# Where in memory the attention and feed-forward activations begin: a two-layer float32 decoder on one core

## The chip, the cores and the metric

One core of one Trainium2 chip runs one program. The metric is the device time of an execution in microseconds, as the median of several runs; lower is better. Engine names are those of the profile: PE is TensorE (PEld are its weight loads), DVE is VectorE, ACT is ScalarE, POOL is GpSimd and SP is SyncE, which issues nearly all transfers.

## The reference

Two layers (`DEPTH = 2`) on 512 tokens of width 1024, all in float32. Each layer is an attention sub-layer and a SwiGLU sub-layer, each with an RMSNorm ahead of it and one behind it:

```
h = rms_norm(x, attn_pre_g[l])
proj = h @ w_in[l]                       # q, k, v of 4 differential heads and 8 forgetting heads
oa = rms_norm(diff_attention(qa, ka, va, lam), diff_sub_g[l]) * (1.0 - lam_init)
ob = forgetting_attention(qb, kb, vb, log_f)
x = x + rms_norm(concat(oa, ob) @ w_out[l], attn_post_g[l])
h = rms_norm(x, ffn_pre_g[l])
y = (silu(h @ w_gate[l]) * (h @ w_up[l])) @ w_down[l]      # D_FF = 2816
x = x + rms_norm(y, ffn_post_g[l])
```

## The kernel before

**Three matmuls for one.** Each float32 operand is split into a high part that is rounded to the matmul's type and a low part with the rest, and each product is the sum of three matmuls (high by high, high by low, low by high). In `mm(out, a, b)` (line 204) `a` is the stationary operand, 128x128, loaded by a weight load (LDWEIGHTS), and `b` the moving one, up to 512 columns wide. A profile row such as `d<-wh_d,hh` names the output and both operands.

**The work of a layer, in order.** `va` (lines 333 to 342) makes the values of the differential heads: the stationary operand is a 128-token slice of the normed input `hT_h` or `hT_l`, the moving one a half-width row block of the weights. Then come the projections `pj_kd`, `pj_qd`, `pj_kf`, `pj_qf` and `vb`, the scores `sd` and `sf`, the transposes of the probabilities `ptd` and `ptf`, and the products with the values, `od` and `of`. A planner (`Plan`) fixes their order at build time; projections and the output projection `o` fill the gaps that the softmax leaves on PE. After that the order is the program's: the output projection's rest, gate and up (`pj_g`, `pj_u`, function `proj_T`: the stationary operand is a weight tile, the moving one `hT_h` or `hT_l`), and down (`d`, function `down_mm`: the stationary operand is a 128-token slice of the hidden activations `hh` or `hl`, the moving one a weight tile). Down has 22 row blocks, 2 halves of the width, 4 token tiles and 3 matmuls each, so 528 matmuls of 512 columns in a layer.

**Weights.** They arrive by a transfer of 512 KB in `wr` (two buffers), ACT writes the high part `wh` and DVE or POOL the low part `wl` (three buffers each). Four rows of down's weights at its end (`TAIL`) lie in free tiles of the feed-forward pool instead (`whl`), and so do the values' weights of the second layer (`wvh`, `wvl`, loaded through `vraw`). In the first layer three quarters of the values' weights lie in tiles of the attention pool (`wva`, `wva0h`, `wva0l`), loaded through `mixd` and `rawv`, and the last quarter in the weight pool (`wh_va`, `wl_va`). Half of the output projection's weights lie in the attention pool too (`wo1h`, `wo1l`), the other half in the weight pool (`wh_o`, `wl_o`).

**Where tiles lie.** A pool is a stretch of SBUF; pools lie one behind the other in the order of their creation, and the attention pool `att{l}` and the feed-forward pool `ffn{l}` take turns in the last stretch. All tiles that matter here are multiples of 512 bytes long in each partition, and a slice of 128 tokens is 512 bytes, so an operand's offset, which here means its start address modulo 512 bytes, is that of its pool. In the compiled program before the change the offsets are:

| tiles | pool | offset |
|---|---|---|
| `xs`, `hT_h`, `hT_l`, the identity in `con` | cpool | 128 |
| `wr`, `wh`, `wl` of all weights | wpool | 384 |
| normed rows `h`, exponentials `ed` and `ae`, `sg` | tpool | 384 |
| `mixd`, `rawv`, `vdh`, `vdl`, `vf`, `wo1h`, `wo1l`, `wva`, `qs`, `ks` | att | 256 |
| `t1`, `t2`, `cb`, `pth`, `ptl` | att | 128 |
| `hh`, `hl`, `whl`, `wvh`, `wvl`, `vraw`, `y0` | ffn | 256 |

The pad tile of `PAD = 8` floats at the end of the small pool `spool` is what puts the last stretch at 256.

Of the kernel before, what the change touches and what calls it, by code (L numbers as in the profile page):

```python
# [11 lines left out]
F32 = mybir.dt.float32  # L12
# [5 lines left out]
P = 128  # L18
# [21 lines left out]
EPS = 1e-6  # L40
BIG = 1e30
MAGIC = 12582912.0
PAD = 8
C_ID, C_M, C_F, NKEEP, C_U = 0, 128, 640, 641, 641
NCONST = 1153
PAIRED = [*range(8, 16), *range(8), *range(16, 32)]
# [127 lines left out]
def hymba_block(ctx, tc, x_d, pos_d, apre_d, win_d, fb_d, lq1_d, lk1_d, lq2_d, lk2_d, dsg_d, wout_d, apost_d,  # L174
# [51 lines left out]
    dsg = cpool.tile([P, DEPTH], F32, name="dsg")  # L226
    spool.tile([P, PAD], F32, name="pad", tag="pad", bufs=1)

# [114 lines left out]
    for l in range(DEPTH):  # L343
        win = win_d[l]
        with ExitStack() as actx:
            ap = actx.enter_context(tc.tile_pool(name=f"att{l}", bufs=1, reuse_waits="tile"))

            def rbuf(tag, dt, name):
                return ap.tile([P, S], dt, name=f"{name}_{l}", tag=tag, bufs=NRC if tag == "rc" else 1)
# [982 lines left out]
```

## Time and profile before

| | us |
|---|---|
| median of 3 runs | 1267.25 (1266.63 to 1270.36) |
| the profiled execution | 1271.73 |
| its span | 1270.0 |
| PE busy in it | 1233.9 (97%) |
| weight loads (PEld) | 1017.4 (80%) |
| DVE, ACT, POOL busy | 635.0 (50%), 520.6 (41%), 279.4 (22%) |

The mean granted clock of TensorE is 0.992 of full speed. The profiled execution took 4.48 us longer than the median; 1.73 us of its time lie outside the span. A matmul's duration in the profile (0.39 us for 512 columns) overlaps that of the next; what counts is the distance from the start of one to the start of the next.

### The profile page before, as it was taken

The numbers are of one execution on the slowest core, as the hardware profiler recorded it, in microseconds if no ns is written. First come the engines' busy times: TensorE is split into PE (matmuls) and PEld (weight loads), VectorE is DVE, ScalarE is ACT, GpSimd is POOL, SyncE is SP. The second block draws the span as 40 slices with busy tenths as digits, with TensorE's granted clock in tenths as the row PEclk, the third lists the DMA queues.
The fourth block names the chain that finished last, engine by engine and source line by source line (L and its number), as shares of the span: only waits on it lengthen the run. The fifth ranks groups of instructions, "written<-read, shape, count | busy, mean of one in ns | idle before, by whom it ended". The sixth has DMA issues, their size and how long they took to land.

```text
span 1270.0 us, 15915 instructions
## 1 busy us (share of the span) xinstructions
PE 1233.9 (97%) x5949; PEld 1017.4 (80%) x5949; DVE 635.0 (50%) x1188; ACT 520.6 (41%) x1008; POOL 279.4 (22%) x318
## 2 busy tenths in 40 slices
PE   8999999999999999999999999999999999999998
PEld 5777887798888888888777878777988888888886
DVE  7597859563333333221556867685633333332224
ACT  5465757453222222222344647674522222221211
POOL 1554557220000000000236535671100000000001
PEclk9999999999999999999999999999999999999999
DMA  7333443404333334223413333432133333332222
GB/s 235 82 84 93 108 116 101 133 18 116 90 94 99 100 100 133 85 97 101 132 34 92 80 95 102 124 128 81 51 100 100 100 92 93 99 117 100 83 100 83
DMA packets 158717, 125.94 MB, mean 99 GB/s; under 512 B 7008, under 2 KB 134112, under 8 KB 158640
## 3 DMA queue, kind: packets, MB, share of 16 engines
q1 hardware_dynamic: 158496, 124.40, 33.0%
q8 instruction: 47, 0.77, 0.2%
q10 hardware_dynamic: 144, 0.52, 0.1%
q14 instruction: 30, 0.25, 0.1%
HBM read 114.32 MB, written 2.20 MB: 92 GB/s over the span
## 4 chain that ended last, share of the span: by engine, by line
PE 55%; issue 31%; DVE 7%; ACT 3%; POOL 3%; DMA 1%; SPq 0%; POOLq 0%; DVEq 0%; ACTq 0%
PE pj_g L204 9%; PE pj_u L204 9%; PE d L204 9%; PE o L204 4%; PE pj_kd L204 4%; PE pj_qd L204 3%; PE va L204 3%; PE vb L204 2%; PE pj_kf L204 2%; PE pj_qf L204 2%; PE sd L204 1%; PE ptf L209 1%; PE sf L204 1%; PE of L204 1%; DVE ae L1032 1%
## 5 line engine op out<-in xcount | busy, mean ns | idle before, releaser
L204 PE MATMUL pj_g<-hT_h,wh_g 128*128 128x512 f32 (+1 forms) x384 | 142.9, 372 | 0.0
L204 PE MATMUL pj_g<-hT_h,wl_g 128*128 128x512 f32 (+1 forms) x384 | 142.6, 371 | 0.0
L204 PE MATMUL pj_g<-hT_l,wh_g 128*128 128x512 f32 (+1 forms) x384 | 142.6, 371 | 0.0
L204 PE MATMUL pj_u<-hT_h,wh_u 128*128 128x512 f32 (+1 forms) x368 | 140.1, 381 | 0.0
L204 PE MATMUL pj_u<-hT_h,wl_u 128*128 128x512 f32 (+1 forms) x368 | 139.8, 380 | 0.0
L204 PE MATMUL pj_u<-hT_l,wh_u 128*128 128x512 f32 (+1 forms) x368 | 139.8, 380 | 0.0
L204 PE MATMUL d<-wh_d,hh 128*128 128x512 f32 x336 | 132.6, 395 | 0.0
L204 PE MATMUL d<-wh_d,hl 128*128 128x512 f32 x336 | 132.6, 395 | 0.0
L204 PE MATMUL d<-wl_d,hh 128*128 128x512 f32 x336 | 132.5, 394 | 0.0
L258 DVE TENSOR_TENSOR wl_u<-wr_u,wh_u 128x1024 fp32r<-128x1024 f32 x44 | 53.9, 1225 | 150.5 <-ACT wh_u L257 150.5
L258 DVE TENSOR_TENSOR wl_d<-wr_d,wh_d 128x1024 fp32r<-128x1024 f32 x42 | 51.5, 1225 | 152.0 <-ACT wh_d L257 151.5
L257 ACT CAST wh_u<-wr_u 128x1024 fp32r<-128x1024 f32 x44 | 46.3, 1052 | 158.4 <-PE pj_g L204 151.7
L257 ACT CAST wh_d<-wr_d 128x1024 fp32r<-128x1024 f32 x42 | 44.1, 1049 | 162.4 <-PE d L204 139.1
L257 ACT CAST wh_g<-wr_g 128x1024 fp32r<-128x1024 f32 x44 | 46.4, 1055 | 145.2 <-issue 124.6
L1205 DVE TENSOR_TENSOR sg<-pj_u,sg 128x512 f32<-128x512 f32 x44 | 30.4, 692 | 140.8 <-PE pj_u L204 140.8
L270 POOL TENSOR_SCALAR v_fp<-s_fp 128x1 f32<-128x1 f32 x8 | 4.1, 508 | 370.4 <-ACT junk L276 370.1
L204 PEld LDWEIGHTS pj_g<-hT_h,wh_g 128*128 128x128 f32 x384 | 72.4, 188 | 12.7
L204 PEld LDWEIGHTS pj_g<-hT_l,wh_g 128*128 128x128 f32 x384 | 72.3, 188 | 12.5
L204 PEld LDWEIGHTS pj_g<-hT_h,wl_g 128*128 128x128 f32 x384 | 72.3, 188 | 12.4
L204 PEld LDWEIGHTS pj_u<-hT_h,wl_u 128*128 128x128 f32 x368 | 69.3, 188 | 13.1
L204 PEld LDWEIGHTS pj_u<-hT_l,wh_u 128*128 128x128 f32 x368 | 69.2, 188 | 13.0
L204 PEld LDWEIGHTS pj_u<-hT_h,wh_u 128*128 128x128 f32 x368 | 69.2, 188 | 13.1
(272 smaller groups left out, 2777.8 us busy)
## 6 DMA issues: line engine op xcount, KB each, us to landing
wr_g<-in_w_gate_dram SPq DMA_DIRECT2D x44, 512.0 KB, 3.8
wr_u<-in_w_up_dram SPq DMA_DIRECT2D x44, 512.0 KB, 3.8
wr_d<-in_w_down_dram SPq DMA_DIRECT2D x44, 512.0 KB, 3.5
wr_o<-in_w_out_dram SPq DMA_DIRECT2D x16, 512.0 KB, 4.2
wr_kd<-in_w_in_dram SPq DMA_DIRECT2D x8, 512.0 KB, 4.0
wr_qd<-in_w_in_dram SPq DMA_DIRECT2D x8, 512.0 KB, 4.1
ksd<-ksd SPq DMA_DIRECT2D x16, 256.0 KB, 2.9
wr_kf<-in_w_in_dram SPq DMA_DIRECT2D x8, 512.0 KB, 4.0
```

Of the source, the lines that this page charges most:

```text
L204: ins = PE.matmul(out, a, b, start=start, stop=stop)
L209: ins = PE.transpose(out, a, idn)
L257: A.copy(hi, raw)
L258: (eng or V).tensor_sub(lo, raw, hi.bitcast(F32))
L270: G.tensor_scalar(v, s2[:, 0:1], scalar1=s2[:, 1:2], scalar2=EPS, op0=ALU.add, op1=ALU.add)
L1032: return V.tensor_scalar_mul(b["e"][:, :n], b["e"][:, :n], b["l"])
L1205: V.tensor_mul(sg, pu, sg)
```

## The change

The pad in `spool` grows from 8 to 104 floats, by 384 bytes, and the attention pool gets a pad tile of 64 floats, 256 bytes, as its first one. Nothing else is changed.

```
-PAD = 8
+PAD, PAD_A = 104, 64
...
             ap = actx.enter_context(tc.tile_pool(name=f"att{l}", bufs=1, reuse_waits="tile"))
+            ap.tile([P, PAD_A], F32, name=f"pad_a{l}", tag="pad")
```

In the compiled program the feed-forward pool then begins at byte 135808 in place of 135424, and its tiles have the offset 128. The attention pool's first real tile begins at 136064 in place of 135424; its tiles that had the offset 256 have 384, and those that had 128 have 256. The other pools stay where they were. Tiles of the two pools now overlap at other places than before, and the order in which instructions are issued is the same on all engines. One wait moves. On DVE, where the second layer's attention begins (`vdl` are the low parts of the values, `t1kd` the first step of the key rotation, `hT_l` the normed input's low part), the rows before are:

```order
L263 TENSOR_TENSOR hT_l<-hp_a_5583,hT_h 128x4x128 [waits Activation_49]
L382 TENSOR_TENSOR vdl_5646<-va_5498,vdh_5645 128x512 [waits DMAHW3_49,Activation_49]
...
L727 TENSOR_TENSOR t1kd_1_5718<-pj_kd_5678,cosT 128x512 [waits DMAHW6_49,PE_49]
L731 STREAM_SHUFFLE t2kd_1_5723<-pj_kd_5678 128x512 [waits DMAHW0_49]
L734 TENSOR_TENSOR t2kd_1_5723<-t2kd_1_5723,sinT 128x512 [waits DVE_49]
```

and with the change:

```order
L263 TENSOR_TENSOR hT_l<-hp_a_5584,hT_h 128x4x128 [waits Activation_49]
L383 TENSOR_TENSOR vdl_5648<-va_5499,vdh_5647 128x512 [waits DMAHW6_49,DMAHW3_49,Activation_49]
...
L728 TENSOR_TENSOR t1kd_1_5720<-pj_kd_5680,cosT 128x512 [waits PE_49]
L732 STREAM_SHUFFLE t2kd_1_5725<-pj_kd_5680 128x512 [waits DMAHW0_49]
L735 TENSOR_TENSOR t2kd_1_5725<-t2kd_1_5725,sinT 128x512 [waits DVE_49]
```

The wait on DMAHW6, which is for the landing of one of the eight `vraw` transfers, moved from `t1kd` to the first `vdl`, four rows earlier.

## Rows read from the trace of the kernel before

**Rows 1.** The page's part 1: engine, busy us, share of the span, instructions.

```profile
PE 1233.9 (97%) x5949; PEld 1017.4 (80%) x5949; DVE 635.0 (50%) x1188; ACT 520.6 (41%) x1008; POOL 279.4 (22%) x318
```

**Rows 2.** Busy time by stretch: gate and up, then down, first layer.

```profile
core 0: us, PE busy (x) PEld busy (x) DVE busy (x) ACT busy (x) POOL busy (x), PEclk, DMA share, GB/s
271.00:513.00 242.00, 242.00 (x1145) 203.61 (x1145) 88.40 (x98) 73.15 (x97) 2.36 (x5) 1.00 0.33 98
513.00:638.00 125.00, 124.52 (x541) 100.78 (x540) 39.70 (x40) 34.58 (x53) 9.55 (x12) 1.00 0.32 102
```

**Rows 3.** The chain of waits, its long pieces: start us, us, what, count.

```profile
242.51 17.42 PE o L204 x75
262.20 4.18 PE o L204 x18
268.65 2.80 PE o L204 x12
...
502.62 5.44 PE pj_g L204 x24
...
513.51 114.33 PE d L204 x492
653.07 11.16 PE va L204 x48
...
870.22 10.48 PE o L204 x45
```

**Rows 4.** Timeline of PE, values of the first layer: start us, us, instruction.

```profile
21.95 0.39 PE L204 MATMUL va<-wva,hT_l 128*128 128x512 f32 x1
...
32.40 0.40 PE L204 MATMUL va<-wva,hT_l 128*128 128x512 f32 x1
32.64 0.40 PE L204 MATMUL va<-wh_va,hT_h 128*128 128x512 f32 x1
...
34.73 0.39 PE L204 MATMUL va<-wh_va,hT_h 128*128 128x512 f32 x1
...
38.13 0.39 PE L204 MATMUL pj_kd<-hT_h,wh_kd 128*128 128x512 f32 x1
```

**Rows 5.** Timeline of PE at the end of the second layer's down.

```profile
1258.71 0.61 PE L204 MATMUL d<-whl,hh 128*128 128x512 f32 x2
1259.16 0.39 PE L204 MATMUL d<-whl,hl 128*128 128x512 f32 x1
1259.39 0.40 PE L204 MATMUL d<-wh_d,hh 128*128 128x512 f32 x1
...
1260.78 0.63 PE L204 MATMUL d<-whl,hh 128*128 128x512 f32 x2
```

**Rows 6.** The chain of waits between the layers, last pieces ahead of PE.

```profile
649.72 0.76 DVE h_a L285
650.48 0.14 issue
650.62 0.63 PE hp_a L209 x4
```

**Rows 7.** Timelines of DVE and PE, last normed rows ahead of the second feed-forward.

```profile
905.28 0.75 DVE L285 SCALAR_TENSOR_TENSOR h_f<-xs,r_f,g_fpre 128x512 f32<-128x512 f32 x1 [1.99 <-POOL r_f L271]
906.93 0.60 PE L209 MATMUL hp_f<-con,h_f 128*128 128x128 f32 x4
```

**Rows 8.** Transfers: their issues with KB each and median us to landing; timelines of users.

```profile
wr_d<-in_w_down_dram SPq DMA_DIRECT2D x44, 512.0 KB, 3.5
ksd<-ksd SPq DMA_DIRECT2D x16, 256.0 KB, 2.9
vraw<-in_w_in_dram SPq DMA_DIRECT2D x8, 256.0 KB, 3.8
51.08 2.17 SPq L709 DMA_DIRECT2D ksd<-ksd  x2
59.45 0.30 PEld L204 LDWEIGHTS sd<-ksd,qsd 128*128 128x128 f32 x2 [1.86 <-issue]
607.42 2.37 SPq L1281 DMA_DIRECT2D vraw<-in_w_in_dram  x4
```

**Rows 9.** The first low part of the second layer's values: duration, first and last start.

```profile
L382 DVE TENSOR_TENSOR vdl<-va,vdh x4: 681/687/693, 660.8 to 664.9; 128x512 fp32r<-128x512 f32 x4
```

## The prediction

> **What bounds the kernel now.** I read first the busy times: PE is busy for 97% of the span and no other compute engine for more than half of it [rows 1]. Then the stretches: in gate and up and in down PE has no gap to speak of, the granted clock is 1.00, and the 16 transfer engines are busy a third of the time [rows 2]. So in the feed-forward the time is the number of matmuls times the distance between two of them. The third view, the chain of waits, gives that distance. A piece of gate and up is 24 matmuls of 512 columns in 5.44 us, 226.7 ns each. Down is 492 matmuls of the same size in 114.33 us, 232.4 ns each [rows 3]. The clock is the same, the other engines and the transfers do no more in down than in gate and up [rows 2], and still every matmul of down takes 5.7 ns longer. The reader should ask what differs: which operand lies where.
>
> The offsets in the table of pools answer it. In gate and up the stationary operand has the offset 384 and the moving one 128. In down it is 256 and 384. The trace holds a direct comparison in one stretch, one loop and one clock, the values of the first layer [rows 4]. From 21.95 us to 32.64 us 46 matmuls read their moving operand from the attention pool (offset 256, stationary operand at 128): 10.69 us, 232.4 ns each. At 32.64 us the same loop goes on with its moving operand in the weight pool (offset 384, stationary still at 128). The first nine take 2.09 us, 232.2 ns each, and the next 15, up to 38.13 us, take 3.40 us, 226.7 ns each. Nothing else changed but the tile. A third case lies at the end of down: with `whl` both operands are in the feed-forward pool, both at 256, and the three from 1258.71 to 1259.39 us take 0.68 us, 226.7 ns each; the six that follow with `wh_d` (256 and 384) take 1.39 us, 231.7 ns [rows 5]. And the output projection, with `wo1h` at 256 moving and 128 stationary, runs at 17.42 / 75 = 232.3 ns [rows 3].
>
> So the rule that the rows show: where the two operands' offsets are equal or 256 apart, a matmul settles at 226.7 ns after about nine; where they are 128 apart, it stays at 232.4 ns on average.
>
> **The change part by part.** It takes no instruction away and adds none; it moves the offsets of two pools. *Down*: stationary from 256 to 128, moving stays at 384, so 256 apart. That is the pair of operand offsets of the 15 fast matmuls in [rows 4]. In each layer 480 matmuls run ahead of the last token loop: 480 x 5.7 ns = 2.74 us, both layers 5.48. In that last loop of the second layer 24 more read `wh_d`: 24 x 5.0 = 0.12 us. In the first layer only the first six of these count, 0.03 us; the rest is covered by the chain of norms, in which PE's transposes wait for DVE's `h_a` up to 650.62 us [rows 6]. Sum 5.6 us, all of it on PE without gaps, so on the path.
>
> *Output projection*: moving `wo1h` and `wo1l` from 256 to 384, stationary 128, 256 apart. The `wh_o` matmuls between them (384 and 128 already) have been thrown out of step by their neighbours; the three long pieces of the first layer, 105 matmuls of both kinds, take 24.40 us, 232.4 ns each [rows 3], and should all settle. 105 x 5.7 = 0.60, with a dozen shorter pieces' matmuls 0.65 us; each restart behind transposes costs 9 x 5.5 = 0.05 us again, about three of them 0.15. So 0.5 us in a layer, 1.0 in both; the second layer's piece runs at 10.48 / 45 = 232.9 ns [rows 3]. DVE's norms must not become the wait: the last `h_f` is ready at 906.03 us and its transpose starts at 906.93 [rows 7]; 0.9 us of slack against a gain of some 0.3 us from the first norm on, so it covers.
>
> *Values, first layer*: 46 matmuls from 256 to 384 moving, 46 x 5.7 = 0.26 us, taken as on the path, since the chain runs through them without a gap. Earlier ones lie among waits for the input and count nothing. *Values, second layer*: `wvh` and `wvl` go from 256 to 128, stationary 128: equal offsets, as for `whl` in [rows 5]. The ones ahead of 653 us lie under the norms [rows 6]; the 48 behind it take 11.16 us, 232.5 ns [rows 3]: 48 x 5.8 less one restart, 0.23 us.
>
> *What stays*: scores have both operands in the attention pool at one offset (256 each, then 384 each), and the products with the values stay 128 apart (256 and 128, then 384 and 256). No row shows these absolute pairs. If only the distance counts they cost 0; if the absolute offset counts too, the nearest rows bound it by 5.7 ns a matmul either way. By the code there are 224 products with the values and 256 score matmuls, most of them narrower than 512 columns: 480 x 5.7 ns, at most 2.7 us given or taken. I take 0, because three pairs at different absolute offsets, (384, 128), (128, 384) and (256, 256), all run at 226.7 ns. *The moved wait*: the last `vraw` was issued by 609.8 us and lands 3.8 us later, 613.6 us; the first `vdl` starts at 660.8 us [rows 8, 9]. It costs 0, and nothing queues behind it. *Transfers* into the moved pools keep their number and size; `wr_d` already lands 512 KB at the offset 384 in 3.5 us, `vraw` 256 KB at 256 in 3.8 us [rows 8], so the offsets show no penalty. The key copies `ksd` are the ones to watch (below).
>
> What comes next when matmuls are faster: a weight chunk of 24 matmuls then lasts 5.44 us in down too. Gate and up live at that rate with the same 512 KB per chunk, the same ACT and DVE work and no gap [rows 2], so the weights keep up.
>
> Sum: 5.6 + 1.0 + 0.26 + 0.23 = 7.1 us. The profiled execution would go from 1271.73 to 1264.6; it stands 4.48 above the median, from which I count: 1267.25 - 7.1 = **1260.1 us**.
>
> **The rivals.** *Nothing changes.* The distance of 232.4 ns could belong to down as such: it changes its output bank every six matmuls, while gate and up stay in one for 24. Against it: in [rows 4] slow and fast ones follow each other with the same six per bank, and `whl` in [rows 5] is fast in down itself. It gives 1267.25. [...] The measured 232.4 against 226.7 ns of one loop speaks against that reading, so this rival gets 0.11.
>
> *Only part arrives.* Down gains its 5.6 us or, if a lock is lost at each of its bank changes, some 4; output projection and values disappear in the softmax's waits. That gives 1261.6 to 1263.3; 0.12. For it: in the attention part PE waits at several places, as for `sd` at 59.45 us [rows 8].
>
> *Slower.* Each key tile has its other half filled by two copies within the attention pool, which land in 2.9 us; the first pair is issued by 51.08 + 2.17 = 53.25 us at the latest, lands by 56.15 and is used at 59.45, so 3.3 us of slack [rows 8]. If a copy at an offset that is no multiple of 256 took more than 2.9 + 3.3 = 6.2 us, every one of 16 key tiles would delay its scores. At 8 us that is 16 x 1.8 = 28.8 us, 1267.25 - 7.1 + 28.8 = 1289 in all; it turns the sign from 6.2 + 7.1 / 16 = 6.6 us on. [...] With `wr_d` at 384 not slow either, this gets 0.05. That the pads do not move the pools as said is excluded by the addresses of the compiled program.
>
> **How the numbers follow.** The forecast in full has 0.72, part of it 0.12, nothing 0.11, slower 0.05. A measurement can tell some 0.3%, 3.8 us, from no change, so faster means below 1263.4. The first two cases lie there, all but a hundredth: 0.83 faster; 0.12 same; 0.05 slower. The range must hold the full case with the bound of 2.7 us, 1260.1 - 2.7 = 1257.4, and the partial case with 0.6 of scatter (as the runs shown lie below their median), 1263.3 + 0.6: 1257.4 to 1263.9. Left out are nothing and slower, 0.16.
>
> **What would show it.** Right: the piece of `d` in the chain falls from 114.33 to about 111.6 us for 492 matmuls, `va` x48 from 11.16 to 10.9, `o` x75 from 17.42 to 17.1, while `pj_g` stays at 5.44 for 24. Wrong: `d` stays at 232 ns with 128 and 384, or settles at another distance; new waits of PE on `ksd`; or the gain of down comes back as a longer wait at `hp_a` or in the softmax.

## The result, and the profile after

| | before | after |
|---|---|---|
| median of 9 runs each, us | 1267.39 | 1261.95 |
| the profiled execution, us | 1271.73 | 1261.95 |
| its span, us | 1270.0 | 1260.1 |
| mean granted clock in it | 0.992 | 0.993 |

The ratio of the runs is 0.9947, with a 95% interval of 0.9924 to 0.9971: faster by 5.4 us. Predicted were 7.1 us and 1260.1 us; the median lies 1.9 us above that and inside the range of 1257.4 to 1263.9. One of the nine runs of after took 3138.16 us and is not in the ratio; no other run of any kernel here came near that, and what happened in it is not known.

The busy times of after answer to [rows 1]. PE is still busy for 97% of the span, with the same 5949 matmuls.

```profile
PE 1223.8 (97%) x5949; PEld 1015.2 (81%) x5949; DVE 633.0 (50%) x1188; ACT 520.8 (41%) x1008; POOL 279.6 (22%) x318
```

The stretches of gate and up and of down in after, with the columns of [rows 2]. The clock and the share of the transfer engines are what they were, and more matmuls fit into the 125 us of the second stretch (541 before, 554 now).

```profile
271.00:513.00 242.00, 242.00 (x1134) 203.12 (x1132) 87.77 (x97) 74.04 (x97) 0.86 (x2) 1.00 0.33 98
513.00:638.00 125.00, 124.09 (x554) 102.00 (x553) 41.66 (x45) 36.54 (x60) 12.87 (x17) 1.00 0.31 101
```

The chain of waits of after, its long pieces (start us, us, what, count), to be laid beside [rows 3].

```profile
21.67 16.37 PE va L204 x72
38.04 5.44 PE pj_kd L204 x24
...
239.54 17.10 PE o L204 x75
...
258.90 4.11 PE o L204 x18
...
265.29 2.75 PE o L204 x12
...
499.27 5.44 PE pj_g L204 x24
...
510.15 111.53 PE d L204 x492
...
646.89 10.91 PE va L204 x48
657.80 5.44 PE pj_kd L204 x24
...
863.51 10.35 PE o L204 x45
```

Down's piece went from 114.33 to 111.53 us: 226.7 ns a matmul, the distance that gate and up have had all along (5.44 / 24). The second layer's values went from 11.16 to 10.91 us, the first layer's output projection from 17.42 + 4.18 + 2.80 to 17.10 + 4.11 + 2.75 us. The first layer's values took 16.65 us before:

```profile
21.64 16.65 PE va L204 x72
```

Second down does not stand in the chain as a piece of its own. Its first and last matmul in the timeline of PE are 119.45 us apart in after:

```profile
1134.07 0.39 PE L204 MATMUL d<-wh_d,hh 128*128 128x512 f32 x1
...
1253.52 0.39 PE L204 MATMUL d<-wh_d,hl 128*128 128x512 f32 x1
```

In before it is 122.38 us, from the same view:

```profile
1140.94 0.40 PE L204 MATMUL d<-wh_d,hh 128*128 128x512 f32 x1
...
1263.32 0.40 PE L204 MATMUL d<-wh_d,hl 128*128 128x512 f32 x1
```

**Where the 9.9 us between the two spans are.** The pieces' starts cut both executions into the same stretches:

| stretch | before | after | difference |
|---|---|---|---|
| start to the first `pj_kd` (values, layer 1) | 38.29 | 38.04 | -0.25 |
| to `o` x75 (attention, layer 1) | 204.22 | 201.50 | -2.72 |
| to down (output projection, gate, up) | 271.00 | 270.61 | -0.39 |
| to `va` x48 (down and norms) | 139.56 | 136.74 | -2.82 |
| to the second `pj_kd` (values, layer 2) | 11.17 | 10.91 | -0.26 |
| to `o` x45 (attention, layer 2) | 205.98 | 205.71 | -0.27 |
| to the end (output projection, gate, up, down) | 399.78 | 396.59 | -3.19 |

The stretches that the prediction has terms for give 0.25 + 0.39 + 2.82 + 0.26 + 3.19 = 6.9 us. (The first of them begins with waits for the input and does not repeat: it is 38.22 us in a second profile of before and 38.40 in one of after. The values' piece in it does: 16.65 in both profiles of before, 16.37 and 16.34 in those of after.) The other 3.0 us lie in the attention parts and cannot be put down to the change: in the second profiles (experiment 1) the first layer's attention takes 197.59 us before and 205.60 after, so the sign is turned round. At 105 us PE of the first profiled execution before waits 2.1 us for DVE's `vf`, and then its granted clock falls to 0.50 of full speed, where 512-column matmuls start 0.43 us apart in place of 0.23 (five distances from 106.61 to 108.74 us). These are the wait, in brackets, and the windows of PE behind it (stretch, its length in us, PE busy (matmuls), granted clock, DMA share, GB/s):

```profile
105.68 0.50 PE L204 MATMUL pj_kd<-hT_h,wh_kd 128*128 128x512 f32 x1 [2.08 <-DVE vf L790]
...
106.00:107.00 1.00, 1.00 (x4) 0.65 0.57 75
107.00:108.00 1.00, 1.00 (x4) 0.50 1.03 366
108.00:109.00 1.00, 1.00 (x4) 0.50 0.24 84
109.00:110.00 1.00, 1.00 (x5) 0.64 0.00 0
```

In the first profiled execution after, PE does not wait there and the clock stays at 1.00. But the second profile of the kernel before has neither the wait nor the fall of the clock:

```profile
107.00:108.00 1.00, 1.00 (x6) 1.00 1.06 378
```

And the second profile of after has both:

```profile
107.28 0.50 PE L204 MATMUL pj_kd<-hT_h,wh_kd 128*128 128x512 f32 x1 [2.06 <-DVE vf L791]
...
109.00:110.00 1.00, 1.00 (x4) 0.50 0.82 289
```

So this is how two executions differ, not two kernels.

### The profile page after: what moved, and what is told of

Same layout as the page of the kernel before. It is cut to its first block, busy times and chain, and to the rows that moved or that the text cites. A ratio compares the mean times of both kernels' runs of the same rounds, so it can differ in the third digit from the quotient of the medians.

```text
span 1260.1 us, 15914 instructions
## 1 busy us (share of the span) xinstructions
PE 1223.8 (97%) x5949; PEld 1015.2 (81%) x5949; DVE 633.0 (50%) x1188; ACT 520.8 (41%) x1008; POOL 279.6 (22%) x318
## 4 chain that ended last, share of the span: by engine, by line
PE 56%; issue 31%; DVE 6%; ACT 3%; POOL 2%; DMA 1%; SPq 0%; POOLq 0%; DVEq 0%; ACTq 0%
PE pj_g L204 10%; PE pj_u L204 10%; PE d L204 9%; PE o L204 4%; PE pj_kd L204 3%; PE pj_qd L204 3%; PE vb L204 3%; PE va L204 3%; PE pj_kf L204 2%; PE pj_qf L204 2%; PE sd L204 2%; PE sf L204 1%; PE ptf L209 1%; PE of L204 1%; DVE ae L1033 1%
```

## The experiments

In all of them "before" is the kernel before, run beside them on the same chip, and a ratio is to that.

**1. Both kernels again.** No edit. The first measurement's interval was wide, and its two profiled executions differed by more than the change.

> The kernel before, unchanged, to see what its executions scatter by. Theory A (the distance of the two operands' offsets sets the distance of two matmuls): 492 matmuls of down in about 114.3 us, 232.4 ns each, and a ratio of 1.000. The clock theory of the scatter: executions with a mean granted clock of 0.992 or 0.993 take some 8 us longer than one at 1.000, since each stretch at half clock costs about 1.6 us and there are five of them; the times then fall on a line against the clock. Rival for the scatter: no relation with the clock.

> The changed kernel, unchanged. Theory A: down 111.5 us for 492 matmuls again, and at equal granted clock 7 us less than the kernel before, so a ratio of 0.9945 to 0.9943. Rival (the gain is 5.4 us, the difference of the two medians, because part of the 7 us is lost in the attention part): 0.9957 at equal clock.

The kernel before again: 1268.32 us, ratio 0.9993 (0.9972 to 1.0014). After again: 1263.05 us, ratio 0.9971 (0.9953 to 0.9989). The chain of waits of the second profile of before:

```profile
506.81 114.33 PE d L204 x492
```

And of after:

```profile
514.62 111.53 PE d L204 x492
```

The pieces repeat to 0.01 us, while the times of one kernel in these 12 runs are spread over 8 us. The granted clock goes with it: the list of runs gives each run's, from 0.986 to 1.000, and over 221 runs of all the kernels here a straight line with one level per kernel has a slope of some -1.06 us for each 0.001 of clock and leaves a scatter of 1.6 us. At the same clock of 0.993 the kernel before comes out at 1268.8 us and the change, over its first 8 and these 12 runs, at 1262.3: 6.5 us, each uncertain by some 0.4. That lies between the 7 us that were expected at equal clock and the 5.4 of the rival, nearer to the first. It is a fit, not a measurement at a held clock, and below "at equal clock" means this fit.

**2. One pool alone.** Which of the two pools' shifts brings what?

```
# feed-forward pool alone at 128; the attention pool stays at 256
-PAD, PAD_A = 104, 64
+PAD, PAD_A = 104, 32
# attention pool alone at 384; the feed-forward pool stays at 256
-PAD, PAD_A = 104, 64
+PAD, PAD_A = 8, 32
```

> Only the feed-forward pool moved (offset 128; the attention pool stays at 256). Theory A: down at 226.7 ns (111.5 us for 492), the second layer's values 10.9 us for 48, while the output projection stays at 232.3 ns (17.4 us for 75) and the first layer's values at 232.4; gain 5.6 + 0.25 = 5.9 us, ratio 0.9954. Rival (the gain needs both pools moved): less than half of that, ratio above 0.998.

> Only the attention pool moved (offset 384; the feed-forward pool stays at 256). Theory A: down stays at 232.4 ns (114.3 us for 492), the output projection and the first layer's values settle at 226.7 ns; gain 0.25 + 2 x 0.5 = 1.2 us, ratio 0.999. Rival (the attention pool's transfers or scores give the gain): most of the 5 to 7 us here, ratio 0.995.

Feed-forward alone: 1262.52 us, ratio 0.9959 (0.9939 to 0.9979). Its chain of waits has down and the second layer's values as after, and the output projection as before:

```profile
239.58 17.42 PE o L204 x75
...
510.57 111.53 PE d L204 x492
...
647.31 10.92 PE va L204 x48
```

Attention alone: 1268.11 us, ratio 1.0019 (0.9999 to 1.0038). Its chain is the mirror image:

```profile
244.11 17.10 PE o L204 x75
...
514.73 114.33 PE d L204 x492
...
654.28 11.16 PE va L204 x48
```

So each shift speeds up just the products whose operand it moves. In the time, though, the attention pool's part cannot be seen: the expected 1.2 us are missing (at equal clock 0.1 us, uncertain by 0.5). The feed-forward's part is the whole measurable gain.

**3. Other offsets, the same distances.** Is it the distance between the operands, or one good address? The kernel before with one pad moves both pools to 384, where down's operands are equal, or to 0, where they are 128 apart again.

```
# both pools at 384
-PAD = 8
+PAD = 40
# both pools at 0
-PAD = 8
+PAD = 72
```

> Both moved pools at the offset 384, with no pad in the attention pool. Theory A (only the distance of the two operands' offsets modulo 256 counts): stationary 384 and moving 384 in down are equal, so down settles at 226.7 ns, 111.5 us for 492; output projection 17.1 us for 75; second layer's values (128 and 384) 10.9 us for 48; the same gain as the change, ratio 0.9945 to 0.996. Rival (the two operands have to lie half of 512 bytes apart, 128 against 384): down stays at 232.4 ns, ratio 0.999.

> Both pools at the offset 0, a multiple of 512. Theory A: weights at 384 and the stationary operand at 0 are 128 apart modulo 256, so down is as slow as before, 232.4 ns, 114.3 us for 492, output projection 17.4 us for 75, ratio 1.000. Rival (a tile's own alignment counts, and a multiple of 512 is the best): down at 226.7 ns or below, ratio 0.995 or less.

Both at 384: 1263.83 us, ratio 0.9955 (0.9931 to 0.998), `d` x492 in 111.53 us. Both at 0: 1268.91 us, ratio 1.0009 (0.9982 to 1.0035), and its chain of waits has before's numbers:

```profile
238.73 17.42 PE o L204 x75
...
509.74 114.33 PE d L204 x492
```

Fast at 128 and 384, slow at 256 and 0, with the weights at 384 each time: the distance decides.

**4. The other operand.** If so, moving the weights must slow gate and up, which no version has touched. A pad at the end of `cpool` shifts every pool behind it by 128: weights at 0, the feed-forward at 256, the attention pool at 0, `hT` still at 128.

```
+    cpool.tile([P, 32], F32, name="pad_c")
```

> The changed kernel with 128 bytes more at the end of the constants' pool, so that all pools behind it move by 128: weights at 0, feed-forward activations at 256, attention at 0, the normed input stays at 128. Theory A: now gate and up are 128 apart and slow, 24 matmuls in 5.58 us in place of 5.44, while down (256 and 0) stays fast, 111.5 us for 492; the projections pj and the output projection are slow too. Gate and up have some 2000 matmuls of 512 columns in both layers, the projections 768: 2000 x 5.7 ns + 768 x 4 ns + output 1 us = 15 us more than the change, so some 8 us more than before, ratio 1.006. Rivals: down as such is slow (gate and up keep 5.44 us); or the offset 256 of the hidden activations is what is slow (down at 114.3 us again).

1276.83 us, ratio 1.0065 (1.0041 to 1.0089). The chain of waits:

```profile
507.19 5.60 PE pj_g L204 x24
...
518.39 111.56 PE d L204 x492
```

For the first time gate and up are slow, 233.3 ns, in a loop that keeps one output bank for 24 matmuls, and down, with hidden activations and weights 256 apart, stays fast beside them (111.56 / 492, 226.7 ns). That is the rival "it belongs to down's banks" turned round, and it ends it. The matmuls of 264 columns among the values `vb`, whose operands moved apart just so, did not slow down: 24 in 2.93 us, and 2.92 in after.

**5. Steps of 32 bytes.** What lies between? A small tile behind every two row blocks of hidden activations puts pair j at the offset 128 + 32 j, while the weights stay at 384.

```
                 V.tensor_mul(sg, pu, sg)
+                if f and f % 2 == 0:
+                    hp.tile([P, 8], F32, name=f"pad_h{l}{f}", tag=f"pad{f}")
                 hh_ = hp.tile([P, S], F32R, name=f"hh{l}{f}", tag=f"hh{f}")
```

> The changed kernel with a pad of 32 bytes between every two row blocks of the hidden activations, so that pair j of 11 has the offset 128 + 32 j against the weights' 384: distances modulo 256 of 0, 32, 64, 96, 128, 160, 192, 224, 0, 32, 64. Theory A in its smooth form: the 24 matmuls of a pair take 5.44 us at distance 0, most (5.58 us) at 128, and something between elsewhere, the same on both sides of 128. In its sharp form: 5.58 us at every distance but 0. Pairs 8 to 10 repeat 0 to 2 and should agree with them.

One run, 1268.52 us. The timeline of PE, first half of the first layer's down: the first matmuls of the pairs 0 to 2 and 6 to 9. From the start of one pair to that of the next are 24 matmuls, and the table below has all of these stretches.

```profile
512.73 0.39 PE L204 MATMUL d<-wh_d,hh 128*128 128x512 f32 x1
518.18 0.39 PE L204 MATMUL d<-wh_d,hh 128*128 128x512 f32 x1
523.77 0.40 PE L204 MATMUL d<-wh_d,hh 128*128 128x512 f32 x1
...
546.18 0.40 PE L204 MATMUL d<-wh_d,hh 128*128 128x512 f32 x1
551.69 0.40 PE L204 MATMUL d<-wh_d,hh 128*128 128x512 f32 x1
557.28 0.39 PE L204 MATMUL d<-wh_d,hh 128*128 128x512 f32 x1
562.73 0.39 PE L204 MATMUL d<-wh_d,hh 128*128 128x512 f32 x1
```

| stationary minus moving, mod 256 | 0 | 32 | 64 | 96 | 128 | 160 | 192 | 224 | 0 |
|---|---|---|---|---|---|---|---|---|---|
| us for 24 | 5.45 | 5.59 | 5.60 | 5.61 | 5.60 | 5.60 | 5.51 | 5.59 | 5.45 |

The fast case is a point: 32 bytes off it the price is already the full one (5.59 us against 5.60 at 128). At 192 the distance is 230 ns, at 64 it is 233, so the sign counts too. Pairs 9 and 10 repeat 1 and 2 (5.59 and 5.60 us), and the second layer's down repeats the order. At the distance 0 the pairs j = 0 and j = 8 give the same 227 ns at two absolute offsets.

**6. The rest of the attention pool.** The addresses of the compiled program show a thing that the table of offsets ahead of the prediction does not: it holds for the first layer. In the second layer `qs`, `ks` and the one of the four `wo1h` and `wo1l` tiles that takes the place of a `ks` (half of `wo1l`) come behind the pool's small tiles, at 128 before and at 256 after. This pad puts all that, and `pth` and `ptl`, at 384.

```
+            ap.tile([P, 32], F32, name=f"pad_b{l}", tag="padb")
```

> The changed kernel with a pad of 128 bytes between the value tiles of the attention pool and its probability tiles, so that pth and ptl lie at 384 as the values do (the products od and of were 128 apart before and with the change). Theory A: an od piece of 12 matmuls falls from 1.88 us to 1.82 or less; 24 heads of od and of in both layers give at most 1.1 us, and since PE waits for the softmax at many places there, 0.3 to 1.1 us reach the end: ratio to before 0.994 to 0.9955. Rival (the products are bound by their start and not by their operands): no change of the piece and the ratio of the change.

1263.6 us, ratio 0.9961 (0.9941 to 0.9981); no gain beyond the change. The products with the values did not shorten, as the rival had it; whether their start is what bounds them, no run shows. The chain of waits of this kernel:

```profile
78.57 1.87 PE od L204 x12
```

and of after, where the two operands are 128 apart:

```profile
77.35 1.88 PE od L204 x12
```

The second layer's output projection did what the addresses say. Distances from one start to the next in ns, the last rows of its long piece, first after and then this kernel:

```
wo1h,hT_h 226 | wo1l,hT_h 234 | wo1h,hT_l 226 | wo1h,hT_h 227 | wo1l,hT_h 234 | wo1h,hT_l 226
wo1h,hT_h 227 | wo1l,hT_h 227 | wo1h,hT_l 226 | wo1h,hT_h 227 | wo1l,hT_h 227 | wo1h,hT_l 226
```

In after only the tile at 256 is slow; at 384 it is not, and the whole piece `o` x45 takes 10.28 us in place of 10.35.

**7. The clock, by filling PE's waits.** If half-clock stretches spread the times, matmuls without use in the waits ahead of them should raise the clock. `KEEP` says how many 512-column matmuls of a constant tile are issued into a score's or transpose's bank ahead of the real ones, which overwrite them. Four places in each layer, with and without the pad of 6, and then the first place alone:

```
+KEEP = {("d", 0, 0, 0): 6, ("d", 1, 3, 0): 7, ("d", 2, 2, 0): 5, ("f", 7, 0): 8}
...
                     b["s"] = bank_s(f"s{name}")
+                    for _ in range(KEEP.get((kind, h, i, m), 0)):
+                        mm(b["s"], upr[:, :P], upr, True, True)
... the same two lines ahead of the transposes, for b["t"]
# the first place alone
+KEEP = {("d", 0, 0, 0): 6}
```

> The changed kernel with 5 to 8 matmuls on a constant, whose results are overwritten, ahead of four matmuls or transposes in each layer that wait 1.2 to 1.9 us for the softmax (at 57, 81, 94 and 227 us of the changed kernel's trace, and their like in the second layer). Clock theory of the scatter: PE is then not idle in these waits, the stretches at half clock that follow them vanish (those behind the wait for a bank at 104 and 724 us stay), the mean granted clock goes from 0.993 to 0.996 or more, and at 1.06 us per thousandth the time falls by 3 to 5 us against the change: ratio to before about 0.992. Rivals: the half clock comes for another reason, and neither clock nor time changes; or the added matmuls delay what waits, and the time rises by up to 1 us.

> Both of the last two together, as the candidate that beats the change: the sum of both gains, a ratio to before of about 0.991. Rival: the two take the same time away and the sum is no better than the better one.

Four places: 1271.82 us, ratio 1.0028 (1.0012 to 1.0044); with the pad 1272.74 us, 1.0033 (1.0015 to 1.005). The mean clock of the runs rose, to 0.9951 and 0.9947 (0.9924 in the 12 runs of experiment 6 on the same chip), and the time rose all the same, by 8.2 and 9.1 us against that kernel. The timeline of PE with the four places shows most of why (the bracket is the wait ahead of a row and what ended it). At the first place the six fill the wait. At the second they wait for the score bank themselves, for DVE's `md`, and then stand in the way of the scores:

```profile
58.83 1.55 PE L205 MATMUL sd<-upr 128*128 128x512 f32 x6
60.41 0.44 PE L205 MATMUL sd<-ksd,qsd 128*128 128x128 f32 x2
...
84.33 1.89 PE L205 MATMUL sd<-upr 128*128 128x512 f32 x7 [1.75 <-DVE md L874]
86.06 1.09 PE L205 MATMUL sd<-ksd,qsd 128*128 128x512 f32 x4
```

There the scores start 1.73 us behind the first added matmul. The third place does the same: 1.22 us of waiting for `md` at 98.35 us, then 1.26 us of added matmuls. In two layers that is 2 x (1.73 + 1.26) = 6.0 us, as an estimate from these rows; the rest of the 8 to 9 us was not followed up.

> The changed kernel with the added matmuls ahead of the first score of each layer alone, the one place of the four where the bank is free and the trace of the last kernels showed that they fit into the wait (the first score stands 1.82 us after the last projection matmul with them, 1.85 without). Clock theory: the stretches at half clock that follow this wait in many executions vanish, the mean granted clock rises by one to two thousandths and the time falls by 1 to 2 us against the change, ratio to before 0.993 to 0.995. Rival: the half clock only moves to the next wait, clock and time stay as with the change.

The first place alone: 1260.51 us, ratio 0.9918 (0.9894 to 0.9942), mean clock 0.9945. Windows of PE behind the first place, in the second profile of after:

```profile
57.00:61.00 4.00, 2.25 (x11) 0.96 0.31 95
61.00:65.00 4.00, 4.00 (x16) 0.61 0.05 18
```

and with the wait filled:

```profile
57.00:61.00 4.00, 3.64 (x17) 1.00 0.33 77
61.00:65.00 4.00, 4.00 (x22) 1.00 0.17 58
```

This pair does not show that filling the wait kept the clock up, because the first profile of after has the same wait unfilled (1.46 us ahead of the score, 1.44 in the second) and its clock did not fall either:

```profile
57.00:61.00 4.00, 2.23 (x12) 1.00 0.28 83
61.00:65.00 4.00, 4.00 (x23) 1.00 0.00 1
```

The first place alone beats the kernel before clearly. Against the change it is not decided: the two were not run beside each other on one chip, its interval overlaps the change's first one, and at equal clock the two are the same (1262.8 and 1262.3 us, uncertain by 0.6 and 0.4), so that what it gains, if it does, is clock. That is not shown either: the mean clock of its 6 runs, 0.9945, is also that of the first 8 runs of after (0.9946).

## Why the prediction was right

**The rule** held for 512-column matmuls in every version: equal or 256 apart, down and gate and up ran at 226.7 ns (111.53 / 492 and 5.44 / 24) and the shorter pieces of values and output projection at 226.9 to 229.2 (16.34 / 72 to 2.75 / 12); 128 apart, the pieces of all of these took 231.7 to 233.3 ns (2.78 / 12 to 5.60 / 24), whichever operand was moved (experiments 2 to 4). The distances in between, of which the prediction says nothing, are nearly all slow too (experiment 5). The rival that nothing changes fell with the first chain of waits. The 24 matmuls of gate and up show it once more: 5.44 us in after and 5.60 in experiment 4, with only addresses changed. Why the distance matters inside the chip no run shows.

**Down**, 5.6 us: the first layer's piece gave 114.33 - 111.53 = 2.80 us, where 2.74 + 0.03 had been counted, the second layer's down 122.38 - 119.45 = 2.93, where 2.74 + 0.12 had been counted. Together 5.7 us; the stretches that hold them in the table above shortened by as much or more (2.82 and 3.19 us), so it is on the path.

**Values**: first layer 16.65 - 16.37 = 0.28 us (0.26 said), second layer 11.16 - 10.91 = 0.25 (0.23 said).

**Output projection**, 1.0 us: this term was too large. The first layer's long pieces gave 24.40 - 23.96 = 0.44 us (0.5 said). The second layer was taken to be like the first, and gave 10.48 - 10.35 = 0.13 us. The step that failed is the one that took the table's 256 for all of `wo1l`: in the second layer half of `wo1l` had been at the fast distance before and is at the slow one after (experiment 6). With that tile moved too the piece takes 10.28 us, 0.07 less, so the change alone is worth 0.44 + 0.13 = 0.6 us in the long pieces, and 0.64 with that tile.

**What stays**: scores and products with the values were put at 0 with a bound of 2.7 us. 12 products take 1.88 us on both sides, bringing them to one offset gave 1.87, and a piece of 4 scores (at 83 us) takes 1.21 on both sides: 0 was right.

**Slower through the key copies**: The waits view of PE has 2.9 us in 2 waits ahead of the scores on both sides that no record explains, and 6.1 us in 5 waits before and 6.5 in 5 after that end with DVE's `md`. In after:

```profile
PE sd L204 <- DVE md L871: 6.5, 5, 1.7
...
PE sd L204 <- issue: 2.9, 2, 1.5
```

Nothing of the 28.8 us of that rival is there.

**Only part arrives** had 0.12. That down would gain only some 4 us if a lock were lost at each change of bank was the author's estimate, and no run shows such a loss: with a change of bank every six matmuls down ran at 226.7 ns (111.53 / 492). Something of the rival is there all the same: the trace holds 6.9 us, the runs gave 5.4 and, the second time, 3.7 us by ratio (0.9971 to 1268.4), with 6.5 at equal clock. The attention pool's part is seen in its pieces (0.28 + 0.44 + 0.13 us) and not in the time of the version that has it alone. Whether waits of the softmax swallow it or the scatter hides it stays open: the measurement can't tell 0.85 us, and the first layer's attention alone differs by 6.6 us between the two profiles of before. So the pieces bear the prediction out. That the median came within 1.9 us of the forecast says less, since the interval of its ratio (0.9924 to 0.9971) is 6 us wide.

**Not foreseen** was why two runs of one kernel differ by up to 1%. The prediction set its profiled execution 4.48 us above the median and carried that over as a plain difference. Waits that come and go and half-clock stretches behind them, such as those at 105 to 109 us, are part of what differs between executions; how much of the 4.48 us each accounts for is not shown.

## What to carry to other kernels

When the same instruction has two distances between starts in two stretches at one clock, compare the addresses of its operands before anything else. In 512-column matmuls of this kernel stationary and moving tiles whose start addresses are equal modulo 256 bytes follow each other some 6 ns sooner (226.7 ns against 232.4 to 233.3 at 128 apart), and pad tiles of 640 bytes in each partition buy that; look up every layer's addresses in the compiled program, since a pool may lay out its tiles differently the second time. To judge a gain under 1%, compare long pieces of the chain, which repeat to 0.01 to 0.03 us, or runs at the same granted clock, and not two spans.

## What the runs showed of the hardware that was not expected

In these runs the distance between 512-column matmuls depends on where stationary and moving operand start relative to each other, modulo 256 bytes: 227 ns at 0, 230 at 192, 233 to 234 at all other steps of 32 (experiment 5). At 264 columns no such difference was seen (2.92 and 2.93 us for 24, experiment 4).

Behind a wait of PE of some 1.5 us the granted clock falls in some executions and not in others, at the same place of the same kernel: behind the wait ahead of the first score the clock of 61 to 65 us is 0.61 in one profile of after and 1.00 in the other. A wait itself can come and go too: the 2.1 us for `vf` at 105 us stand in one of two profiles of each kernel. Over a whole execution each 0.001 of mean clock goes with some 1.06 us (the line through 221 runs in experiment 1).

Matmuls without use that fill a wait are not free where they wait for the same thing as the real ones: the first of the four places, filled alone, cost nothing that could be measured, at the second and third the added matmuls waited for `md` and came on top, and all four together cost 8 to 9 us.
